# Row-wise maximum norm of a 67-million-element matrix: a tail of 24 rows instead of 16, its last two rows loaded in turns, and another order of two waits

## The chip, the cores and the metric

The kernel runs on one core of a Trainium2 chip. The metric is the device time of one execution in microseconds (us). Before the change it is 626.84 us, the median of three runs (626.80 to 626.91).

## The reference

```python
x = np.random.randn(8192, 8192).astype(np.float32)
np.linalg.norm(x, ord=np.inf, axis=1)
```

For a matrix and `axis=1` this is the largest absolute value of each row: 268.4 MB are read from HBM, and 8,192 floats are written. There is one comparison for each element and nothing else to compute.

## The kernel before, in words

The matrix is cut into 64 rows for each of the 128 partitions. A row lies along a partition's free dimension, so a row's norm is one reduction on VectorE (called DVE in the profile): `absmax` (line 240) is a maximum with absolute values over the last axis. SyncE (SP) issues all loads, on one queue and in program order; ScalarE's queue issues one store.

There are two stages.

- **The bulk.** 48 rows of each partition are loaded in 24 loads (line 252) of 2 rows each, 128 x 16,384 floats or 8.4 MB. Each load is followed by one reduction that leaves two row results in `r_bulk`.
- **The tail.** The last 16 rows of each partition are one stretch of 131,072 columns, and the list `TAIL` (line 20) cuts it into 33 loads whose width shrinks from 13,440 to 512 columns (line 286). A load may end in the middle of a row. Each load is then cut into `pieces` at the row ends (lines 259 to 266), one reduction a piece. A piece that isn't a row's last leaves a partial maximum, one column wide. The row's last piece is reduced together with the partials (line 299), which have been written just ahead of its data, so that both are one stretch of memory; its result goes to `r_tail`. Where a load holds a row's last piece and the start of the next row, the reduction of the later piece is issued first (line 293).

All loads go into one `ring` of three slots of 16,384 columns and 512 columns more, 49,664 in all (line 217). Bulk load number i (from 0) goes to slot i modulo 3. The tail begins in the slot that follows the bulk's last (line 270), and each tail load is put behind the one before it, with room for the partials of its first row in front, rounded up to 128 columns; a load that would pass the ring's end goes to the front (lines 276 to 278). A load into a stretch of the ring must wait for the reductions that still read what lies there. These waits are put in by the framework from the overlaps: DVE counts its finished instructions in one semaphore, and each load waits for a value of it. Each load signals its landing on one of eight semaphores in turn, so that a load also waits until the eighth load before it has landed. On each engine the instructions run in program order, so a load that waits holds back all loads behind it on SP.

The bulk's results are stored from ScalarE's queue (line 305), after the reductions of the third-last tail load; the tail's results are stored by SP at the very end (line 307).

Some functions then edit the finished program. `drop_implied_waits` (line 129) removes waits that another wait implies. For a DVE instruction that waits both for a landing and for DVE's own counter (`counter`), it drops the counter's wait if the load that landed had itself waited for that value (lines 168 to 171); otherwise the instruction keeps both. An instruction holds one wait itself; a second one becomes an instruction of its own ahead of it. The other functions move the first load to the program's very start and shorten its opening and its end; the change doesn't touch them.

Of the kernel before, what the change touches and what calls it, by code (L numbers as in the profile page):

```python
# [17 lines left out]
HEAD, STEP = 32, 8  # L18

TAIL = [  # L20
# [5 lines left out]
]  # L26


# [91 lines left out]
def rewait(i, waits):  # L120
    return copy.replace(
        i,
        sync_info=mybir.SyncInfo(
            on_wait=waits, on_update=list(i.sync_info.on_update)
        ),
    )


def drop_implied_waits(nc):

    sp, dve = mybir.EngineType.SP, mybir.EngineType.DVE
    body = nc.main_func.blocks[-2]
    insts = list(body.instructions)
    counter, seen, upto = None, {}, []
    for i in insts:
        if i.engine != dve or i.sync_info is None:
            continue
        for s in i.sync_info.on_wait:  # L140
            assert s.sync_type == "semaphore" and s.wait_mode == "sem-ge-imm"
            seen[s.id] = max(seen.get(s.id, 0), s.wait_value)
        for s in i.sync_info.on_update:
            assert s.update_mode in ("sem-inc", "sem-add-imm")
            assert counter in (None, s.id)
            counter = s.id
            upto += [dict(seen)] * s.update_value
    behind, total = {}, {}
    for n, i in enumerate(insts):
        if i.sync_info is None:  # L150
            continue
        waits = i.sync_info.on_wait
        own = max([s.wait_value for s in waits if s.id == counter], default=0)
        if type(i).__name__ == "InstDMACopy":
            (up,) = i.sync_info.on_update
            total[up.id] = total.get(up.id, 0) + up.update_value
            behind[up.id, total[up.id]] = own
            if i.engine == sp and own and len(waits) > 1:
                known = upto[own - 1]
                insts[n] = rewait(  # L160
                    i,
                    [
                        s
                        for s in waits
                        if s.id == counter or s.wait_value > known.get(s.id, 0)
                    ],
                )
        elif i.engine == dve and own and len(waits) > 1:
            past = max(behind.get((s.id, s.wait_value), 0) for s in waits)
            if past >= own:  # L170
                insts[n] = rewait(i, [s for s in waits if s.id != counter])
    body.instructions = insts


# [27 lines left out]
@with_exitstack  # L202
def kernel(
    ctx: ExitStack,
    tc: tile.TileContext,
    x: bass.AP,
    out: bass.AP,
    G: int = 4,
    B: int = 2,
    SLOTS: int = 3,  # L210
    PAD: int = 128,
):
    nc = tc.nc
    P = nc.NUM_PARTITIONS
    rows, cols = x.shape
    W = B * cols
    R = SLOTS * W + PAD * 4


    n_tail = sum(TAIL) // cols  # L220
    assert sum(TAIL) == n_tail * cols
    n_bulk_rows = rows // P - n_tail
    assert n_bulk_rows % (G * B) == 0
    A = n_bulk_rows // (G * B)
    split = n_bulk_rows * P
    x_b = x[:split].rearrange("(a p n b) c -> a n p (b c)", p=P, a=A, n=G, b=B)
    out_b = out[:split].rearrange("(a p n b) -> p a (n b)", p=P, a=A, n=G, b=B)
    x_t = x[split:].rearrange("(p t) c -> p (t c)", p=P)
    out_t = out[split:].rearrange("(p t) -> p t", p=P)

    pool = ctx.enter_context(tc.tile_pool(name="sbuf", bufs=1))
    r_bulk = pool.tile([P, A, G * B], F32)
    r_tail = pool.tile([P, n_tail], F32)
    used = [HEAD, A * G * B, n_tail]
    gap = -sum(-(-n // STEP) * STEP for n in used) % PAD
    pool.tile([P, gap], F32, name="gap")
    ring = pool.tile([P, R], F32)

    def absmax(o, i):
        return nc.vector.reduce_max(  # L240
            out=o, in_=i, axis=X, apply_absolute_value=True
        )

    def after(ins, first, kind):
        info = mybir.DependencyInfo(kind, mybir.DependencyReason.SCHED_ONLY)
        tc.add_manual_dep(ins.ins, first.ins.name, info, reason="order")

    for a in range(A):
        for n in range(G):
            at = (a * G + n) % SLOTS * W  # L250
            t = ring[:, at : at + W]
            nc.sync.dma_start(out=t, in_=x_b[a, n])
            absmax(
                r_bulk[:, a, n * B : (n + 1) * B],
                t.rearrange("p (b c) -> p b c", b=B),
            )


    pieces, at = [], 0
    for j, w in enumerate(TAIL):  # L260
        end = at + w
        while at < end:
            r = at // cols
            to = min(end, (r + 1) * cols)
            pieces.append((j, r, to - at))
            at = to
    of_row = [[k for k, s in enumerate(pieces) if s[1] == r] for r in range(n_tail)]


    here = A * G % SLOTS * W  # L270
    start, slot = [], []
    for j, w in enumerate(TAIL):
        first = next(s for s in pieces if s[0] == j)
        ks = of_row[first[1]]
        n_part = len(ks) - 1 if pieces[ks[-1]][0] == j else 0
        at = -(-(here + n_part) // PAD) * PAD
        if at + w > R:
            at = -(-n_part // PAD) * PAD
        start.append(at)
        slot.append(at - n_part)  # L280
        here = at + w

    src = 0
    for j, w in enumerate(TAIL):
        at = start[j]
        nc.sync.dma_start(out=ring[:, at : at + w], in_=x_t[:, src : src + w])
        src += w
        here = [k for k, s in enumerate(pieces) if s[0] == j]
        offs = [at + sum(pieces[i][2] for i in here[:m]) for m in range(len(here))]
        todo = list(zip(here, offs))  # L290
        if slot[j] != at:

            todo = todo[1:] + todo[:1]
        for k, lo in todo:
            _, r, n = pieces[k]
            ks = of_row[r]
            if k == ks[-1]:
                frm = slot[j] if len(ks) > 1 else lo
                done = absmax(r_tail[:, r : r + 1], ring[:, frm : lo + n])
            else:  # L300
                to = slot[pieces[ks[-1]][0]] + ks.index(k)
                done = absmax(ring[:, to : to + 1], ring[:, lo : lo + n])
        if j == len(TAIL) - 3:

            ins = nc.scalar.dma_start(out=out_b, in_=r_bulk[:])
            after(ins, done, mybir.DependencyClass.Sync)
    nc.sync.dma_start(out=out_t, in_=r_tail[:])
    nc.at_finalize(drop_implied_waits)
    nc.at_finalize(start_first_load_early)
    nc.at_finalize(finish_on_pool)  # L310
    nc.at_finalize(open_without_vector)
# [30 lines left out]
```

## Time and profile before

| What | Before |
|---|---|
| Median of three runs | 626.84 us |
| Span of the profiled execution | 624.4 us (624.41) |
| What lies around that span, up to the median | 2.43 us |
| DVE busy | 552.8 us in 71 instructions |
| Bulk reductions | 24 of 17.22 us, with 70.8 us of idle time ahead of them |
| Tail reductions | 31 that leave partials, 91.6 us; 16 that end a row, 50.2 us |
| Data moved | 268.47 MB, 430 GB/s over the span |

The profile records one execution. Its span runs from the first to the last recorded instruction of the program. Busy times are those of the engines; a wait is idle time, and the profile names what ended it. A load is a DMA: its issue is an instruction of SP, and its landing is seen some time later, when its semaphore has its value. The page shows the span in 40 slices of 15.6 us, with a digit for the busy tenths of each. A stretch of the span can be asked for by itself: the length, the busy time of each engine, the share of the DMA engines' time and their rate in GB/s. The timeline lists instructions by start and length in us; several of one kind are merged into one line with their number.

### The profile page before, as it was taken

To read this page: it belongs to the slowest core of one execution; us is meant where nothing else is said; L and a number is where in the kernel's file an instruction comes from. 1 tells how busy PE (TensorE), PEld (TensorE's weight loads), DVE (VectorE), ACT (ScalarE), POOL (GpSimd) and SP (SyncE) were. 2 spreads that over 40 slices of the span, in tenths; PEclk is the share of its full clock that TensorE was granted. 3 is DMA by queue.
4 is the path that set the end of the run, shared out by engine and by line. 5 is a ranking of instruction groups with operands and counts; after the bars stand their busy time and mean duration, and the time that the engine had idled before them with its cause. 6 is when DMAs were issued, how large, how long until landed. Compare 5 with 4: busy or idle time off the path is not lost.

```text
span 624.4 us, 161 instructions
## 1 busy us (share of the span) xinstructions
DVE 552.8 (89%) x71; POOL 0.2 (0%) x4
## 2 busy tenths in 40 slices
DVE  0588988889988899888898888988889999999999
POOL 0000000000000000000000000000000000000000
DMA  9999999999999999999999999999999999999998
GB/s 403 462 411 453 420 445 428 403 470 403 470 403 462 411 453 420 432 441 403 470 403 470 403 466 407 458 416 449 424 439 429 422 438 430 428 429 424 430 424 343
DMA packets 8993, 268.47 MB, mean 430 GB/s; under 512 B 1696, under 2 KB 1696, under 8 KB 3616
## 3 DMA queue, kind: packets, MB, share of 16 engines
q1 hardware_dynamic: 8208, 268.44, 99.6%
q10 hardware_dynamic: 784, 0.02, 0.1%
q14 instruction: 1, 0.01, 0.0%
HBM read 268.44 MB, written 0.03 MB: 430 GB/s over the span
## 4 chain that ended last, share of the span: by engine, by line
DMA 58%; DVE 41%; another core or an unknown queue 0%; issue 0%
DMA ring<-in_x_dram 58%; DVE r_bulk L240 25%; DVE ring L240 10%; DVE r_tail L240 6%
## 5 line engine op out<-in xcount | busy, mean ns | idle before, releaser
L240 DVE TENSOR_REDUCE r_bulk<-ring 128x2 f32<-128x16384 f32 x24 | 413.3, 17220 | 70.8 <-DMA ring<-in_x_dram 70.8
L240 DVE TENSOR_REDUCE ring<-ring 128x1 f32<-128x512 f32 (+20 forms) x31 | 91.6, 2997 | 0.0
L240 DVE TENSOR_REDUCE r_tail<-ring 128x1 f32<-128x8192 f32 (+12 forms) x16 | 50.2, 3143 | 0.0
L326 POOL MEMSET const-bfloat16-1.0<- 128x1 bf16 x1 | 0.1, 101 | 0.0
L326 POOL MEMSET const-uint8-127<- 128x1 uint8 x1 | 0.1, 101 | 0.0
L326 POOL MEMSET const-float32-0.0<- 128x1 f32 x1 | 0.1, 98 | 0.2 <-issue 0.2
L326 POOL MEMSET const-float32-1.0<- 128x1 f32 x1 | 0.1, 98 | 0.0
## 6 DMA issues: line engine op xcount, KB each, us to landing
ring<-in_x_dram SPq DMA_DIRECT2D x1, 6720.0 KB, 37.3
ring<-in_x_dram SPq DMA_DIRECT2D x1, 6400.0 KB, 33.0
ring<-in_x_dram SPq DMA_DIRECT2D x1, 5760.0 KB, 27.2
ring<-in_x_dram SPq DMA_DIRECT2D x1, 5120.0 KB, 39.0
ring<-in_x_dram SPq DMA_DIRECT2D x1, 4544.0 KB, 36.0
ring<-in_x_dram SPq DMA_DIRECT2D x1, 4096.0 KB, 32.1
ring<-in_x_dram SPq DMA_DIRECT2D x1, 3648.0 KB, 40.4
ring<-in_x_dram SPq DMA_DIRECT2D x1, 3264.0 KB, 36.4
```

The costliest lines, as they stand in the source:

```text
L240: return nc.vector.reduce_max(out=o, in_=i, axis=X, apply_absolute_value=True)
L326: nc = _bacc.Bacc("TRN2", target_bir_lowering=False, num_devices=1)
```

## The change

The change has three parts.

- `TAIL` becomes a list of pairs, the column where a load starts and its width, so that the order of the loads is free. It covers 24 rows (196,608 columns) in 37 loads instead of 16 rows in 33. The bulk has 40 rows in 20 loads. The loads' total is 57 in both.
- The last two rows, 22 and 23 (columns 180,224 to 196,608), are loaded in turns from the load at column 188,416 on: a load of the one, then a load of the other. Their two row ends are the last two loads.
- In `drop_implied_waits`, a DVE instruction that keeps both waits now has them sorted so that the landing's comes first in the list and the counter's last. In the finished program the wait for DVE's counter then stands ahead as an instruction of its own, and the reduction itself holds the wait for the landing; before, it was the other way round. In the kernel with the change this concerns two instructions, the last two reductions. In the kernel before there are two with both waits as well, one of them the last.

```diff
 TAIL = [
-    13440, 12800, 11520, 10240, 9088, 8192, 7296, 6528,
-    5760, 5248, 4608, 4096, 3712, 3328, 2944, 2688,
-    2304, 2048, 1920, 1664, 1536, 1408, 1280, 1152,
-    1024, 896, 768, 768, 640, 640, 512, 512,
-    512,
+    (0, 15872), (15872, 16384), (32256, 16384), (48640, 16000),
+    (64640, 14336), (78976, 12800), (91776, 11392), (103168, 10112),
+    (113280, 9088), (122368, 8064), (130432, 7296), (137728, 6528),
+    (144256, 5760), (150016, 5248), (155264, 4608), (159872, 4096),
+    (163968, 3712), (167680, 3328), (171008, 2944), (173952, 2688),
+    (176640, 2432), (179072, 2176), (188416, 1920), (181248, 1792),
+    (190336, 1536), (183040, 1408), (191872, 1280), (184448, 1152),
+    (193152, 1024), (185600, 896), (194176, 768), (186496, 768),
+    (194944, 640), (187264, 640), (195584, 512), (187904, 512),
+    (196096, 512),
 ]
...
             if past >= own:
                 insts[n] = rewait(i, [s for s in waits if s.id != counter])
+            else:
+                insts[n] = rewait(
+                    i, sorted(waits, key=lambda s: s.id == counter)
+                )
...
-    pieces, at = [], 0
-    for j, w in enumerate(TAIL):
+    pieces = []
+    for j, (at, w) in enumerate(TAIL):
         end = at + w
...
-    src = 0
-    for j, w in enumerate(TAIL):
+    for j, (src, w) in enumerate(TAIL):
         at = start[j]
         nc.sync.dma_start(out=ring[:, at : at + w], in_=x_t[:, src : src + w])
-        src += w
```

The sum of the tail's widths is now taken from the pairs, and an assertion checks that they cover the stretch without a gap.

More of the change, by code (lines that the diff above doesn't have):

```diff
@@ L217 @@
     R = SLOTS * W + PAD * 4
-    n_tail = sum(TAIL) // cols
-    assert sum(TAIL) == n_tail * cols
+    n_tail = sum(w for _, w in TAIL) // cols
+    met = 0
+    for lo, w in sorted(TAIL):
+        assert lo == met
+        met += w
+    assert met == n_tail * cols
     n_bulk_rows = rows // P - n_tail
@@ L271 @@
     start, slot = [], []
-    for j, w in enumerate(TAIL):
+    for j, (_, w) in enumerate(TAIL):
         first = next(s for s in pieces if s[0] == j)
@@ L281 @@
         here = at + w
-    src = 0
-    for j, w in enumerate(TAIL):
+    for j, (src, w) in enumerate(TAIL):
         at = start[j]
         nc.sync.dma_start(out=ring[:, at : at + w], in_=x_t[:, src : src + w])
-        src += w
         here = [k for k, s in enumerate(pieces) if s[0] == j]
```

## The prediction

> **What bounds the kernel now.** First I read the 40 slices and the costliest groups of the page: they tell the loads from the reductions.
>
> ```profile
> DVE  0588988889988899888898888988889999999999
> DMA  9999999999999999999999999999999999999998
> L240 DVE TENSOR_REDUCE r_bulk<-ring 128x2 f32<-128x16384 f32 x24 | 413.3, 17220 | 70.8 <-DMA ring<-in_x_dram 70.8
> ```
>
> The DMA engines are full from end to end. In the bulk VectorE (DVE) takes 17.22 us for a load that arrives every 19.33 us (its starts stand at 408.85, 428.14, 447.44 in the timeline) and waits 2.1 us each time: the bulk is bound by the transfers. From slice 30 on, in the tail, DVE is full as well. Next the stretches (length, DVE busy, POOL busy, clock, DMA share, GB/s):
>
> ```profile
> 22.00:466.00 444.00, 396.05 (x23) 0.00 (x0) 1.00 1.00 433
> ...
> 484.00:560.00 76.00, 76.00 (x15) 0.00 (x0) 1.00 0.99 428
> 560.00:600.00 40.00, 39.97 (x15) 0.00 (x0) 1.00 1.00 429
> 600.00:612.00 12.00, 12.00 (x7) 0.00 (x0) 1.00 1.01 424
> 612.00:620.00 8.00, 8.00 (x9) 0.00 (x0) 1.00 1.02 413
> ```
>
> From 484 on both are bound: DVE never rests, and the transfers run near their bulk pace, losing a few per cent only where the loads are small. The chain of waits agrees: it runs through one load from 552.84 to 592.28, and then through DVE alone to the end. Then the timeline of the end (start, length, what), and how long the last load and the last store took from issue to landing:
>
> ```profile
> 621.65 1.27 DVE L240 TENSOR_REDUCE ring<-ring 128x1 f32<-128x512 f32 x2
> 622.36 0.41 ACTq L305 DMA_DIRECT2D out_dram<-r_bulk  x1
> 622.95 0.70 DVE L240 TENSOR_REDUCE r_tail<-ring 128x1 f32<-128x522 f32 x1
> 623.67 0.35 SPq L307 DMA_DIRECT2D out_dram<-r_tail  x1
> ```
>
> ```profile
> ring<-in_x_dram SPq DMA_DIRECT2D x1, 256.0 KB, 6.5
> ...
> out_dram<-r_tail SPq DMA_DIRECT2D x1, 8.0 KB, 1.4
> ```
>
> The last load, issued at 616.14, lands at 622.64. The last reduction starts 0.31 us later, ends at 623.65, and releases the store. So 1.01 us lie between the last landing and the end of the work. This execution has a span of 624.41 us, and 2.43 us more lie around it up to the median of 626.84 (the store lands at 625.1, past the span's end). I take those 2.43 as unchanged. About 0.2% (1.25 us) is what a measurement of this kernel can tell from no change.
>
> **The change, part by part.**
>
> *Eight more rows in the tail.* The number of loads stays (24+33 = 20+37 = 57), and so do the bytes. Four bulk loads of 16,384 columns become tail loads of 15,872, 16,384, 16,384 and 16,000; from 7,296 columns down the sizes are the old ones but for four (2,432, 2,176, 1,920, 1,792 for 2,304, 2,048, 1,920, 1,664). A load of 16,384 takes 19.33 us, 1.180 ns a column; the tail's 131,072 columns took 622.64-466.79 = 155.85 us, 1.2 us above that pace, nearly all in the small loads, which stay. So 0.0 for the pace of the transfers.
>
> *In the tail one partition's data begin 24 rows (768 KB) behind the last one's and not 16 (512 KB).* Neither pitch costs by a row of before: the bulk at 8 rows (256 KB) runs at 433 GB/s, the first tail loads at 428 to 435. I take 0; the ends are 0 and -1.2 (the whole excess of the tail). The Trainium skill, "DMA: Bandwidth & Descriptors", section "Latency and other measured facts", reports copies at a row pitch of 512 KiB at 207 GB/s, and a padded pitch as the cure; by that the change takes the tail off a bad pitch. The trace speaks against it with 428 GB/s at that very pitch.
>
> *The ring at the seam.* This is the part that I weigh most. With 24 bulk loads the tail starts in slot 0; with 20 it starts in slot 2 (20 modulo 3). The first tail load fills elements 32,768 to 48,640. The second, 16,384 wide, doesn't fit behind it (the ring ends at 49,664), wraps, leaves 128 elements for its row's one partial, and covers 128 to 16,512: slot 0 and the first 128 elements of slot 1. So SP can't issue it before DVE has finished with slot 1, the 20th bulk load; until then nothing later can be issued either, SP's queue being in order. In the timeline of before:
>
> ```profile
> 389.55 17.22 DVE L240 TENSOR_REDUCE r_bulk<-ring 128x2 f32<-128x16384 f32 x1 [2.16 <-DMA ring<-in_x_dram]
> 406.80 19.63 SPq L252 DMA_DIRECT2D ring<-in_x_dram  x2
> 408.85 17.22 DVE L240 TENSOR_REDUCE r_bulk<-ring 128x2 f32<-128x16384 f32 x1 [2.08 <-DMA ring<-in_x_dram]
> ```
>
> The 20th reduction ends at 406.77, so the second tail load goes out at 406.80. The load ahead of it, the only one in flight, lands 512 columns (0.60 us) before the 408.83 of the load in its place now: at 408.22. An issue onto an idle queue is dear. The store at the end bounds it from below: 1.4 us from issue to landing. The first load bounds it from above: issued at 0.00, it lands at 22.02, which is 2.69 us over its 19.33.
>
> ```profile
> 0.00 39.61 SPq L252 DMA_DIRECT2D ring<-in_x_dram  x4
> ...
> 22.04 17.22 DVE L240 TENSOR_REDUCE r_bulk<-ring 128x2 f32<-128x16384 f32 x1 [22.04 <-DMA ring<-in_x_dram]
> ```
>
> The second load's landing slips by 406.80 + price - 408.22: nothing at 1.4, 1.27 us at 2.69. I take 1.7 and +0.28: the row nearest is the store's, since that queue is warm as this one is, while the first load's packets began spread from 1.0 to 2.1 us after its issue, a matter of the program's start; the 0.3 is my estimate for the read from HBM that the store hasn't got (0.14 of it is seen: first packets 0.99 us after issue there, 0.85 at the store). The Trainium skill, same page, section "Anatomy of one DMA", has a fit of 2.0 us fixed cost, for DMAs issued by GpSimd; at 2.0 the slip would be 0.58. What slips here is not caught up: every later landing waits in the same queues. The next loads are covered: the third waits for the first piece (8.67 us) of the first, done at about 416.9, ten us ahead of the second's landing; the following ones have a whole load in flight besides.
>
> *Eight more reductions (79 for 71).* A reduction of w columns costs w/960 + 0.14 us, and back-to-back ones overlap by 0.08 (two of 0.674 take 1.27 at 621.65): 0.06 us for each split, 0.48 in all. I count it as hidden: in the four wide tail loads DVE needs 17.3 us per 19.3 us of transfer, so it reaches the shrinking loads with nothing behind it, where before it came 1.3 us late (13,440 columns landed at 482.64, DVE began at 483.95). Uncovered it would cost the 0.48.
>
> *The last two rows in turns, and the order of the two waits.* Before, the last row-end reduction reads a partial that the reduction just ahead of it writes: it starts 0.03 after that one's end (622.92) and not 0.08 before it: 0.12 us. After, its newest partial is two instructions old. And the row ends leave the small loads: from the load of 1,920 on, each is one reduction. Its pitch, w/960 + 0.06, summed over 1,920, 1,792, 1,536 and so on to the last but one (519 wide, with its partials) gives 16.30 us; the landings of the loads behind them, with intervals as now (0.64 us for 512, 1.23 for 1,024, 2.28 for 1,920), take 16.37. So a lag of some 0.16 behind the landings at the load of 1,920 (worked on from the landing at 592.28, where DVE started 0.02 behind) falls to 0.09, where it is now 0.2 to 0.3 from the load of 1,152 on. The last reduction, 519 wide, takes 0.68: 0.09+0.68 = 0.77 us from landing to end for 1.01, a gain of 0.24. If DVE is free, 0.02+0.68 gives a gain of 0.31; if it lags as now, nothing. The order of the two waits, which moves the wait for DVE ahead and leaves the DMA's on the instruction, concerns two instructions, the last two. An instruction that holds its own DMA wait starts 0.02 after a landing (592.28 to 592.30); one whose wait stands ahead of it started 0.31 after, most of it owed to the partial. I put its share inside the 0.24.
>
> *Stores.* The bulk's results are 20 KB and not 24, off the path (landed at 624.36, before the tail's). The tail's are 96 bytes a partition and not 64, on the path: 0, at most 0.05.
>
> *Instruction fetch.* The page has one packet of an instruction queue; it ran at 587.5, on one DMA engine, and the load under way took 4.31 us for 3,328 columns instead of 3.93. With 11 more instructions it moves or comes twice: 0, at most 0.4 either way.
>
> **Sum:** +0.28 - 0.24 = +0.04 on the 623.65 at which the work ended, so 626.84 + 0.04, **626.9 us**.
>
> **The rivals.** *The queue never runs dry* (price under 1.45 us): for it, the store's 1.4; against it, a load moves 8 MB and reads HBM first. Then -0.24 to -0.31: 626.6. Chance 0.26. *The cold price* (slower): the seam costs all 2.69 - 1.42 = 1.27 us; for it, the only load onto an idle queue in the trace; against it, that queue was cold. With the end's gain 1.03, 627.9; without it 1.27, 628.1, past the 0.2% bound from a price of 2.67 on. Chance 0.16, of which 0.06 lies beyond the bound. *DVE is the bound* in the tail, as its full slices say: the eight splits cost 0.48, with the seam hidden behind them: 627.3; against it, the idle time of 2 us at each of the first four tail loads. Chance 0.07. *The end doesn't change* (the waits do nothing, the lag stays): +0.28, 627.1. Chance 0.05. *The pitch* mattered after all: -1.2 + 0.04 = -1.16, 625.7, and -1.44 with the queue fed too; against it, 428 GB/s. Chance 0.04, half of it past the bound. The forecast itself, 626.7 to 627.2, has 0.42.
>
> The range of 626.4 to 627.9 holds the forecast, the queue that stays fed, DVE as the bound, the unchanged end and the near part of the cold price: some 0.85. Faster by over 0.2%: half of the pitch, 0.02. Slower: 0.06. Within: 0.92.
>
> **What would show it.** Issue of the second tail load at 406.8 (not 387.4), and its landing later than 19.33 us after the first's: the difference is the seam. A dip in the slice of the DMA row there. From the last landing to the last reduction's end 0.77 us, not 1.01. DVE idle for about 2 us at the first tail loads. I would be wrong in kind if the second load goes out 20 us earlier, if a later load also meets an empty queue, or if the small loads land at another pace than now.

## The result, and the profile after

The kernel with the change takes **628.12 us**, the median of 10 runs (627.87 to 629.01), beside 626.88 for the kernel before (626.61 to 627.42): a ratio of 1.0022, 95% interval 1.0014 to 1.0030. It is slower by 1.24 us, clear of the noise. The profiled execution has a span of 625.78 us for 624.41, 1.37 us longer; it took 628.44 us in all.

Two lines of the groups of the page after (count, then busy time and mean length, then idle time before and what ended it):

```profile
L253 DVE TENSOR_REDUCE r_bulk<-ring 128x2 f32<-128x16384 f32 x20 | 344.4, 17220 | 62.1 <-DMA ring<-in_x_dram 62.1
L253 DVE TENSOR_REDUCE r_tail<-ring 128x1 f32<-128x8192 f32 (+14 forms) x24 | 85.9, 3585 | 9.7 <-DMA ring<-in_x_dram 9.5
```

VectorE now waits in the tail too: 9.5 us, where the tail had no idle time before. The timeline of the kernel after tells where (start, length, instruction, idle time before it):

```profile
389.26 17.22 DVE L253 TENSOR_REDUCE r_bulk<-ring 128x2 f32<-128x16384 f32 x1 [2.14 <-DMA ring<-in_x_dram]
406.51 40.35 SPq L298 DMA_DIRECT2D ring<-in_x_dram  x4
407.98 8.69 DVE L253 TENSOR_REDUCE r_tail<-ring 128x1 f32<-128x8192 f32 x1 [1.49 <-DMA ring<-in_x_dram]
416.58 8.14 DVE L253 TENSOR_REDUCE ring<-ring 128x1 f32<-128x7680 f32 x1
429.17 8.69 DVE L253 TENSOR_REDUCE r_tail<-ring 128x1 f32<-128x8192 f32 x1 [4.45 <-DMA ring<-in_x_dram]
```

The last bulk reduction ends at 406.48, and the second tail load is issued right behind it, at 406.51, as the prediction read from the ring. The first tail load lands at 407.95, the second at 429.14. That is 21.19 us later, where a load of this width follows another in 19.33: a slip of 1.86 us. The chain of waits has a new piece there, and it is the load that was issued late:

```profile
406.49 0.02 issue
406.51 22.64 DMA ring<-in_x_dram
429.14 0.02 issue
429.17 8.69 DVE r_tail L253
```

At the end, the timeline again:

```profile
623.74 1.28 DVE L253 TENSOR_REDUCE r_tail<-ring 128x1 f32<-128x519 f32 x2
623.85 0.41 ACTq L316 DMA_DIRECT2D out_dram<-r_bulk  x1
625.05 0.35 SPq L318 DMA_DIRECT2D out_dram<-r_tail  x1
```

The last two row ends follow each other with an overlap of 0.08 us. The last load lands at 624.29, its reduction starts 0.04 us later and ends at 625.02: 0.73 us from landing to end, for 1.01 before.

So the trace's account is: last landing 624.29 for 622.64, +1.65; from there to the end of work -0.28; together +1.37, the difference of the spans. Of the +1.65 the slip at the seam makes 1.86. In this execution the bulk ran 0.27 us ahead of the one before (first tail load landed at 407.95, where 408.22 was expected), and 0.06 is left over for the rest of the tail.

### The profile page after: what moved, and what is told of

Same layout as the page of the kernel before. It is cut to its first block, busy times and chain, and to the rows that moved or that the text cites. A ratio compares the mean times of both kernels' runs of the same rounds, so it can differ in the third digit from the quotient of the medians.

```text
span 625.8 us, 169 instructions
## 1 busy us (share of the span) xinstructions
DVE 553.3 (88%) x79; POOL 0.2 (0%) x4
## 4 chain that ended last, share of the span: by engine, by line
DMA 55%; DVE 44%; issue 0%; DVEq 0%
DMA ring<-in_x_dram 55%; DVE r_bulk L253 19%; DVE ring L253 16%; DVE r_tail L253 9%; DVEq L348 0%
## 5 line engine op out<-in xcount | busy, mean ns | idle before, releaser
L253 DVE TENSOR_REDUCE r_bulk<-ring 128x2 f32<-128x16384 f32 x20 | 344.4, 17220 | 62.1 <-DMA ring<-in_x_dram 62.1
L253 DVE TENSOR_REDUCE ring<-ring 128x1 f32<-128x7680 f32 (+26 forms) x35 | 125.9, 3636 | 0.0
L253 DVE TENSOR_REDUCE r_tail<-ring 128x1 f32<-128x8192 f32 (+14 forms) x24 | 85.9, 3585 | 9.7 <-DMA ring<-in_x_dram 9.5
```

The lines of the kernel that those rows point to most:

```text
L253: return nc.vector.reduce_max(out=o, in_=i, axis=X, apply_absolute_value=True)
```

## The experiments

The theory after the result: the whole loss is the seam, where one load is issued onto a queue that runs dry, at a higher price than predicted. The rivals: the 24-row tail costs by itself (its pitch, or its eight more reductions), or the end's gain has another source than the change's order. A number behind the slip is always the landing of the load minus that of the load ahead, minus 19.33 us. The lead is how long before the landing of the load ahead the issue takes place.

### Without the seam

```diff
-    (0, 15872), (15872, 16384), (32256, 16384), (48640, 16000),
+    (0, 15872), (15872, 16256), (32128, 16384), (48512, 16128),
```

> The kernel after, with the second tail load 128 columns narrower (16,256, so that it lies in slot 0 alone and doesn't touch slot 1) and the fourth 128 wider. Theory (the seam): the second load is issued some 19 us earlier, at about 387, with a load in flight; its landing comes 19.2 us behind the first's instead of 21.2; the end moves forward by the 1.86 us of the slip, less what the tail had made up (0.2), so 1.65 to 1.9 us under the kernel after and 0.2 to 0.6 us under the kernel before (626.3 to 626.7). Rival (the tail of 24 rows as such costs, by its pitch or by its 79 reductions): the issue moves, but the time stays within 0.3 us of the kernel after's 628.1.

Measured: 626.65 us (11 runs, 626.56 to 627.31), 0.9992 of the kernel before (0.9983 to 1.0001). The timeline of this kernel:

```profile
387.38 57.53 SPq L298 DMA_DIRECT2D ring<-in_x_dram  x4
389.50 17.22 DVE L253 TENSOR_REDUCE r_bulk<-ring 128x2 f32<-128x16384 f32 x1 [2.15 <-DMA ring<-in_x_dram]
408.20 8.69 DVE L253 TENSOR_REDUCE r_tail<-ring 128x1 f32<-128x8192 f32 x1 [1.48 <-DMA ring<-in_x_dram]
416.81 8.14 DVE L253 TENSOR_REDUCE ring<-ring 128x1 f32<-128x7680 f32 x1
427.34 8.69 DVE L253 TENSOR_REDUCE r_tail<-ring 128x1 f32<-128x8192 f32 x1 [2.39 <-DMA ring<-in_x_dram]
```

With 128 columns less, the second load is issued at 387.38 and not 406.51, and VectorE's wait for it is 2.39 us and not 4.45; the landing comes 19.14 us behind the first's (16,256 columns). The tail has the same pitch of 24 rows and the same 79 reductions, and none of the loss is left. The rival falls: neither pitch nor reductions cost anything that shows.

The kernel after and this one were then run once more, on one chip.

> The kernel after, unchanged, on one chip with the next: its seam again. In the profile the second tail load is issued 1.4 to 1.5 us before the first lands and lands 20.9 to 21.6 us behind it (slip 1.6 to 2.3); the time is 1.0 to 1.6 us above the kernel before's. If the slip is the same each time, it is a price; if it differs by 0.5 us or more from 1.86 with the same lead, it is a draw about a price.

> The kernel of the first experiment (second load 16,256 wide, no seam), beside the kernel after on one chip: 1.3 to 1.7 us under it, and 0.1 to 0.5 us under the kernel before, if the seam is all that the change lost.

Measured: the kernel after 628.22 us (11 runs), ratio 1.0021 (1.0012 to 1.0030); without the seam 626.67 (11 runs), ratio 0.9996 (0.9987 to 1.0005). The difference is 1.55 us. In the second profile of the kernel after the lead is 1.44 us again and the slip 1.83 for 1.86, so in the two profiles it is a price rather than a draw.

### The order of the waits alone, and the old order without the seam

```diff
             if past >= own:
                 insts[n] = rewait(i, [s for s in waits if s.id != counter])
+            else:
+                insts[n] = rewait(
+                    i, sorted(waits, key=lambda s: s.id == counter)
+                )
```

> The kernel before with the new order of the two waits alone. Theory (what the last reduction waits for is the partial of the one just ahead of it): it still starts 0.03 us after that one's end, so from the last landing to the end of work 0.9 to 1.0 us and no time gained, within 0.1 us. Rival (the wait for the landing, standing alone, delayed the last reduction): 0.1 to 0.25 us gained between landing and end.

Measured: 627.14 us (11 runs), ratio 1.0001 (0.9992 to 1.0010). From the last landing (622.89) to the end of work (623.95) it is 1.06 us, no better than the 1.01 before. The timeline:

```profile
621.88 1.27 DVE L244 TENSOR_REDUCE ring<-ring 128x1 f32<-128x512 f32 x2
...
623.25 0.70 DVE L244 TENSOR_REDUCE r_tail<-ring 128x1 f32<-128x522 f32 x1
```

The reduction ahead ends at 623.15, and the last one starts 0.10 us behind that: with the wait for the counter standing ahead as an instruction of its own, it starts 0.07 us later behind that end than it did with the wait on itself.

The other way round, the kernel without the seam lost the same four lines:

> The kernel of the first experiment with the old order of waits (the landing's wait alone ahead, DVE's on the reduction). Theory: the last two reductions follow closely (lag 0.05 to 0.1 us behind the landing), so the order is worth at most 0.1 us here. Rival (the order is what gives the end's gain): from the last landing to the end 0.95 us or more, as before the change, and 0.2 to 0.3 us slower than the first experiment.

Measured: 626.69 us (11 runs), ratio 0.9995 (0.9987 to 1.0004); 0.85 us from landing to end, beside 0.78 and 0.83 in the two profiles with the new order. The order shows in neither kernel's time, and in the traces it is worth less than 0.1 us either way.

### The last two rows one after the other

The kernel without the seam, with the columns from 179,072 on in their natural order and the widths as they are.

```diff
-    (176640, 2432), (179072, 2176), (188416, 1920), (181248, 1792),
-    (190336, 1536), (183040, 1408), (191872, 1280), (184448, 1152),
...
+    (176640, 2432), (179072, 2176), (181248, 1920), (183168, 1792), (184960, 1536),
+    (186496, 1408), (187904, 1280), (189184, 1152), (190336, 1024),
...
```

> The kernel of the first experiment (second load 16,256 wide, no seam) with the last two rows loaded one after the other, widths unchanged. Theory (the turns keep the row end and the partial just written away from the last reduction): the last reduction waits for the one ahead of it again and lags by 0.2 to 0.3 us; from the last landing to the end of work 0.95 to 1.05 us instead of 0.72, the time 0.2 to 0.3 us above the first experiment's. Rival (the gain at the end came from DVE reaching the small loads early, thanks to the 24 rows): 0.7 to 0.8 us as in the first experiment.

Measured: 627.34 us (11 runs, 626.69 to 627.66), ratio 1.0007 (0.9998 to 1.0016). The last landing is at 622.18, and the timeline goes on:

```profile
621.79 0.68 DVE L252 TENSOR_REDUCE ring<-ring 128x1 f32<-128x512 f32 x1
622.58 0.70 DVE L252 TENSOR_REDUCE r_tail<-ring 128x1 f32<-128x522 f32 x1
```

The last reduction starts 0.11 us after the one that writes its partial, and 1.09 us lie between landing and end. With the turns it is 0.78 and 0.83 us, so the turns give about 0.3 us (some 0.07 of it is the new order's own loss where a partial has just been written, as above), and the rival that credits the earlier start of the tail falls. The two kernels' times were not taken side by side, and the intervals of their ratios overlap; the reading rests on the profiles. The medians differ by 0.69 us, more than the 0.2 to 0.3 expected, and what the rest of it is wasn't found.

### The price of an issue onto an empty queue

```diff
-    SLOTS: int = 3,
+    SLOTS: int = 1,
```

> The kernel before with a ring of one slot: every bulk load waits for the reduction of the load ahead of it, so that all 24 go onto an empty queue. Measures the price of such an issue, 24 times. Theory (the price of a wide load is that of the seam): from issue to landing 22.0 to 22.7 us each, that is 2.7 to 3.3 over the 19.33 of a load that follows another, and the whole kernel about 24 x (22.3+17.3) + 160, some 1,120 us. Rival (the price in a warm queue is near the store's 1.4, and the seam's 3.3 was something else): about 20.7 to 21.1 us each. A third possibility is a wide spread between loads: then the price is a draw, and so is the seam.

In so small a ring the partial maxima of several tail rows get the same place (element 127), and one is written over another before it is read, so that some tail rows come out otherwise. The bulk, which is what is read here, is complete.

Measured: 1,197.9 us (one run), 78 us more than estimated: behind the bulk's last reduction the tail takes another 254 us, 112 of them waits of VectorE, where the estimate had 160. The DMA view (number, median us from issue to landing):

```profile
ring<-in_x_dram SPq DMA_DIRECT2D x24, 22.0
```

The 23 bulk loads issued behind a finished reduction, 17.3 us after the queue ran dry, land 21.78 to 22.19 us after their issue: a price of 2.45 to 2.86 us over 19.33. So a warm queue is no cheaper than the program's first load (2.69), and the store's 1.4 us was the wrong row. Yet the seam's price, 22.64-19.33 = 3.31, lies above all 24. The trace's packets show where the price lies. In the steady stream a packet of 64 KB takes 2.42 us, and each of the 16 DMA engines moves eight of them for a load of this width. At the seam 15 of the engines' first packets take 2.88 to 3.44 us, and the last engine begins 2.94 us after the issue; in the one-slot run the first ones of load 5, for one, take 2.82 to 3.26 and all have begun by 1.56 us. The latest of the first packets ends 5.40 us after the issue at the seam (5.37 in the second profile, where the last engine begins at 2.25), and 4.6 to 4.8 us after it in the one-slot run. From there to the landing it is 17.2 us at the seam and 17.2 to 17.4 in the one-slot run: so the difference is made by the first packets, and the seven behind them cost the same.

### How the slip goes with the lead

Four kernels move the lead. Two change the first tail load's width:

```diff
-    (0, 15872), (15872, 16384), (32256, 16384), (48640, 16000),
-    (64640, 14336),
+    (0, 14336), (14336, 16384), (30720, 16384), (47104, 16384),
+    (63488, 15488),
```

> The kernel after with the first tail load 14,336 wide instead of 15,872 (the columns go to the fourth and fifth loads), the seam as it is. The first load lands 1.8 us earlier, so the second, still issued at 406.5, finds a queue that has been dry for 0.3 us. Theory (the slip is the price of an issue less the lead that it has, with the 2.5 to 2.9 us of the one-slot run for a dry queue): the second lands 19.33 + 2.8 to 3.2 us behind the first, and the time is 1.0 to 1.4 us above the kernel after's. Rival (the seam's own 3.3 us holds whatever the queue does): 3.6 us, and 1.8 above.

```diff
-    (0, 15872), (15872, 16384), (32256, 16384), (48640, 16000),
+    (0, 16256), (16256, 16384), (32640, 16384), (49024, 15616),
```

> The kernel after with the first tail load 16,256 wide (384 columns more, taken from the fourth), the seam as it is. The first lands 0.45 us later, so the second's issue leads by 1.9 us instead of 1.45. Theory (price less lead, with the 3.3 us of the seam): a slip of 1.4 us, the time 0.45 us under the kernel after's. Rival (with a price of 2.7): a slip of 0.8. Third possibility (the slip is a matter of the queue having run empty at all, not of the lead): 1.8 again.

One puts a narrow load ahead of the late one:

```diff
-    (0, 15872), (15872, 16384), (32256, 16384), (48640, 16000),
+    (0, 15872), (15872, 896), (16768, 16384), (33152, 16384), (49536, 15104),
```

> The kernel after with a load of 896 columns between the first and the second, put into the room behind the first (it waits for nothing new), and the columns behind it moved on; the fifth load is 15,104 wide. The wide load that wraps is still issued at 406.5, but the queue ahead of it now lasts 1.09 us longer: lead 2.5 us, with two loads in flight and not one. Theory (the lead is what counts, at a price of 3.3 to 3.5): a slip of 0.8 to 1.0 us, the time 0.7 to 1.0 under the kernel after's. Rival (a lead under 3 us saves nothing sure, since the price grows with it, as between the runs with a dry queue and with 1.9 us of lead): a slip of 1.5 to 3 us, and no gain.

And one puts a seam into the kernel before:

```diff
             at = (a * G + n) % SLOTS * W
+            if a * G + n in (22, 23):
+                at += PAD
```

> The kernel before with bulk loads 22 and 23 (from 0) shifted by 128 columns, so that load 22 touches slot 2 and waits for the reduction of load 20 instead of 19: one seam, with a lead of 2.05 us, in a kernel that is otherwise the old one. Theory (any such seam costs, whatever the tail): load 22 lands 20.5 to 22.3 us behind load 21 (slip 1.2 to 3.0), and the time is 1 to 3 us above the kernel before's. Rival (the slip needs the kernel after's tail, its pitch of 24 rows or its loads): 19.33 us and no change.

Measured, with the kernel after and the one-slot run:

| Kernel | Lead, us | Slip, us | Price (lead + slip) | Median time, us (runs) |
|---|---|---|---|---|
| one slot | dry for 17.3 | | 2.45 to 2.86 | |
| first load 14,336 | -0.39 | 3.32 | 2.93 | 630.99 (4) |
| after, two profiles | 1.44 | 1.86, 1.83 | 3.30, 3.27 | 628.12 (10), 628.22 (11) |
| first load 16,256 | 1.90 | 1.64 | 3.54 | 628.54 (10) |
| seam in the bulk | 2.00 | 2.36 | 4.36 | 629.19 (4) |
| narrow load between | 2.49 | 2.83 | 5.32 | 628.52 (10) |
| without the seam | 20.8 | none | | 626.65 (11), 626.67 (11) |

The timelines of the 14,336 and of the narrow load between show the late landing as VectorE's wait, 7.26 and 5.40 us:

```profile
428.76 8.69 DVE L253 TENSOR_REDUCE r_tail<-ring 128x1 f32<-128x8192 f32 x1 [7.26 <-DMA ring<-in_x_dram]
```

```profile
431.19 8.69 DVE L253 TENSOR_REDUCE r_tail<-ring 128x1 f32<-128x8192 f32 x1 [5.40 <-DMA ring<-in_x_dram]
```

The seam in the bulk, in the old kernel:

```profile
425.74 0.81 SPq L254 DMA_DIRECT2D ring<-in_x_dram  x2
427.77 17.22 DVE L240 TENSOR_REDUCE r_bulk<-ring 128x2 f32<-128x16384 f32 x1 [2.05 <-DMA ring<-in_x_dram]
449.46 17.22 DVE L240 TENSOR_REDUCE r_bulk<-ring 128x2 f32<-128x16384 f32 x1 [4.47 <-DMA ring<-in_x_dram]
```

A seam put into the old kernel costs as well (629.19, ratio 1.0036, 1.0022 to 1.0049), so it needs nothing of the new tail. And "price less lead" with one price fails: in these kernels a lead of 1.9 to 2.5 us left slips of 1.64 to 2.83, on the whole no less than the 1.83 and 1.86 at a lead of 1.44, for the price grows about as fast as the lead. The kernels with the first load of 16,256 and with the narrow load between vary most from run to run (627.47 to 630.01 and 627.07 to 629.22), so their slips in one profile are draws. The time of the 14,336 holds something besides the slip: VectorE falls behind on the changed widths, with 1.79 us from the last landing to the end. Its time lies 2.87 us above the kernel after's, where 1.0 to 1.4 was expected, and its slip of 3.32 is also above the expected 2.8 to 3.2.

### Many seams in one run

```diff
-    SLOTS: int = 3,
+    SLOTS: int = 2,
```

> The kernel before with a ring of two slots: from the third bulk load on, each is issued when the reduction of the load two ahead ends, with one load in flight, which lands about 2.1 us later. Measures 22 seams in a row. Theory (price less lead): with a price P over 2.06 the loads come every 19.33 + (P-2.06)/2 us, so 19.65 with P = 2.7 and 19.95 with P = 3.3, in all 7 to 14 us more than before over the bulk. Rival (an issue 2 us ahead of the landing is early enough, and the seam's slip had another cause): 19.33 us as before, the time within 1 us of 627.

Measured: 659.59 us (one run), 33 us above the kernel before; the bulk's idle time on VectorE is 96.2 us for 70.8, and the tail, which had none, has 6.7 us. The loads don't come evenly. The timeline:

```profile
39.33 83.64 SPq L252 DMA_DIRECT2D ring<-in_x_dram  x5
41.37 17.22 DVE L240 TENSOR_REDUCE r_bulk<-ring 128x2 f32<-128x16384 f32 x1 [2.07 <-DMA ring<-in_x_dram]
63.70 17.22 DVE L240 TENSOR_REDUCE r_bulk<-ring 128x2 f32<-128x16384 f32 x1 [5.11 <-DMA ring<-in_x_dram]
83.13 17.22 DVE L240 TENSOR_REDUCE r_bulk<-ring 128x2 f32<-128x16384 f32 x1 [2.21 <-DMA ring<-in_x_dram]
105.39 17.22 DVE L240 TENSOR_REDUCE r_bulk<-ring 128x2 f32<-128x16384 f32 x1 [5.04 <-DMA ring<-in_x_dram]
```

The first late load (lead 2.02) slips by 3.00 us. That leaves the next one a lead of 5.06, and it slips by 0.10; then comes a lead of 2.16 and a slip of 2.93. Seven loads in this run have a lead of 5.0 to 5.4 us, and their slips are 0 to 0.65. Both theories miss: the loss is larger than "price less lead" allows, and it comes on some loads alone. Of the bulk loads with a lead of 2.0 to 2.7, seven slip by 2.9 to 3.4 us and eight by 0 to 0.5. The seven have prices of 5.0 to 5.7 us; the eight have 2.4 to 2.7, which is what a dry queue cost above, and their lead counts in full. Followed packet by packet, six of the eight were issued when 12 to 15 of the 16 engines had already run dry, and a few late engines had set the landing ahead. So the landing of the load ahead says little where the engines are out of step. But that isn't the whole rule: at the other two of the eight no engine had run dry, and neither had one at six of the seven.

What remains open is why an issue into the last 2.7 us of a load mostly costs more than one onto a queue that is quite dry, and what decides between the dear and the cheap ones. The packets tell that the latest of the engines' first packets start later and some take longer; whether that comes from how a load's parts are handed to the engines or from the reads of 16 engines that start together wasn't tried.

## Why the prediction was wrong

The forecast was 626.9 us, no change, with a range to 627.9; the time is 628.12.

- **The seam** was found, in its place and with its issue time (406.8 foretold, 406.51 measured, and the bulk of that execution was 0.27 ahead). The step that failed is the price: "I take 1.7 and +0.28: the row nearest is the store's, since that queue is warm as this one is". The price is 3.3, and the term +1.86 instead of +0.28. No run shows the 0.3 us that was put on top of the store's 1.4 for the read from HBM: the one-slot run's loads lie 1.0 to 1.4 us above the store. The choice of the row was wrong: the one-slot run gives 2.45 to 2.86 for every warm issue of a load, so the first load's 2.69 was the right row, and its slow start no matter of the program's beginning. And the upper end was wrong too: 2.69 was measured on a dry queue, and I took for granted that an issue before the queue runs dry can cost no more than one after it. The runs show that it can: by 0.4 to 2.5 us in the kernels with one such seam, by 2.2 to 2.9 in seven loads of the two-slot run, and not in eight others of that run. Had the range taken only the first load's row it would still have missed by 0.6 us at the seam.
- **The pace of the tail and its pitch**: 0 forecast, and nothing measured that shows: without the seam the last load lands at 622.38 and 622.70 in the two profiles, for 622.64 before. The prediction drew too much from the Trainium skill here: the row on the pitch ("DMA: Bandwidth & Descriptors", "Latency and other measured facts") gives 207 GB/s at 512 KiB for copies between HBM tensors, in each direction, and 214 as the full rate. So by that row 512 KiB is hardly a bad pitch, and its 207 can't be set beside the 428 GB/s of loads into SBUF; no run here copies between HBM tensors. In these runs the move from a pitch of 512 KB to one of 768 KB gave no gain.
- **Eight more reductions**: hidden, as forecast. VectorE waits 1.49, 4.45, 1.99 and 1.58 us ahead of the first four tail loads; without the seam 1.48, 2.39, 2.10 and 1.73.
- **The end**: -0.24 forecast, -0.28 measured (0.73 us from landing to end; 0.77 foretold). It comes from the turns (0.3 us), and the order of the waits has no measurable share.
- **Instruction fetch**: one packet again, at 557.4, one engine; no difference.
- **The rivals**: "the cold price", slower, with a chance of 0.16, is the one that came about, and past its own price. "The queue never runs dry", 626.6, is what the kernel without the seam measures: 626.65. (Its condition should have been a price under 1.42 us, 408.22 less 406.80, and not 1.45; nothing hangs on it.)
- **The signs**: the issue, the late landing, the 0.73 us at the end and VectorE's waits at the first tail loads came as listed. The dip in the slices' DMA row didn't: the row reads 9 at the seam as elsewhere.

In sum the mechanism was right and one term was mis-sized by 1.6 us, which is more than all other terms together.

## What to carry to other kernels

When a change moves a ring's phase, write down for every load which slot it touches, by a single element too, and how long the queue still lasts when it can be issued; here 128 columns of overlap cost 1.55 us, and 128 columns less won it back. A lead of 1.4 to 2.7 us before the queue's last landing can't be counted on: twelve of twenty such issues here still slipped by 1.6 to 3.4 us, and eight, all in the two-slot run, by 0 to 0.5. Take the price from a load of the same size, not from a small store. Rows that end in turns keep a partial result from being read by the very next reduction, and that was worth 0.3 us at the end of the chain.

## What the runs showed of the hardware that was not expected

- Eight-megabyte loads onto a dry queue land 2.45 to 2.86 us later than in a stream, 23 times out of 23. Issued 1.4 to 2.7 us before the last landing, twelve had prices of 3.3 to 5.7 us, and eight, in one run, 2.4 to 2.7. At leads of 5.0 to 5.4 us the slip was 0 to 0.65, at 10 us or more none was seen.
- In the kernel after, no packet of the late load starts for 0.95 us from its issue, and the first packets of 15 engines take 2.88 to 3.44 us instead of 2.42. The load lands 17.2 us after the latest of the first packets ends.
- An instruction that waits for the result of the one just ahead started 0.03 us after its end with the wait on itself, and 0.10 us after it with the wait as an instruction ahead.
